# GpSimd instead of transfers for 80 low halves, one queue for the later transfers, and chunk ends taken bank by bank

## The chip, the cores and the metric

The kernel runs on one core of one Trainium2 chip. The metric is the device time of one execution in microseconds (us), median of three runs. The engines are TensorE (PE, with its weight loads as PEld), VectorE (DVE), ScalarE (ACT), GpSimd (POOL) and SyncE (SP). SP, ACT and POOL also issue the transfers (DMA), each in the order of its own queue.

## The reference, cut to what matters

One layer over 512 tokens of width 2048, in float32. `h = RMSNorm(x)` goes through one projection of width 13712 that feeds three branches and their gates. A is a sparse attention (an indexer picks 128 keys for each query, 8 heads), B a latent attention (8 heads, causal), C a cross-attention into 256 memory tokens (4 heads). Then:

```python
u = jnp.stack([o_a * silu(az), o_b * silu(bz), o_c * silu(cz)], axis=2)
y_br = jnp.einsum('bsnw,nwd->bsnd', u, w_branch[l])
g = jax.nn.sigmoid(gates.reshape(bsz, seq, N_BRANCH, d))
merged = jnp.einsum('bsnd,bsnd->bsd', g, y_br)
x = x + merged @ w_out[l]
```

## The kernel before, in words

**Halves.** Every large matmul is made from fp32r operands in two parts, a high half (the value rounded) and a low half (what the rounding left): high·high, high·low and low·high are summed, so each product is three matmuls. Activations are split once and kept; the weights are streamed in pieces of 128x1024 values (two rows of 128, 512 columns), called `wraw`, `sraw` or `so` when they land, and split into `whi` (an ACT copy) and `wlo` (source minus `whi`, on DVE). For the six silu-gate chunks of 512 columns (`w_in`, columns AZ, BZ, CZ; here "z chunks") and the first two of the three branch products, `wlo` is made otherwise (`halves_by_dma`): ACT writes minus `whi` into `wlo`, and a transfer on the POOL queue adds the same weights from DRAM to it (`accum_op`). There are 48 + 32 such pieces.

**The stream.** `stream` is the main line of matmuls. It walks jobs, one for each piece of weights: a plain chunk job is 2 rows x 4 banks x 3 = 24 matmuls of 512 columns, a Strassen job 12. Before a job's matmuls it prepares (`prep_upto`) up to three jobs ahead (`LOOK`), so `whi` and `wlo` have four buffers and `wraw` three, and issues on SP the load of the next piece whose buffer is let go. A plain chunk accumulates in the four banks of the ring `pg`; its last job ends them, `evac` empties each (ACT and DVE), and the next chunk opens the same four banks. Within a job the order is row, then bank.

**The order of the stages.** Memory keys and values, `iq0`, then the Strassen chunks of the projection and the merge gates (to about 878 us), `iq1`, the latent expansions `uq` and `ukv`, the z chunks, the branch products in the order C, B, A (`branch_chunk`, i = 0, 1, 2), and the output projection (`out_chunk`). Beside them run threads (`c_thread`, `c_part`, `b_thread`, `b_part`, `idx_thread`, `a_bias_thread`, `a_thread`, `u_thread`), Python generators that name what they wait for. All instructions are put in order at build time: `run` lets the stream emit a few matmuls and then lets each thread go on whose wait is over by the clock of `Plan`, a table of costs for each engine and queue. PE then executes that order strictly. A begins when B has ended (`a_bias_thread`, `a_prepare`: fourteen loads for positions, bias table, keys and values); the branch product i = 2 needs A's result through `u_thread` and `gate`.

**Queues.** Weight loads and the loads of `u_thread` are on SP. Spilled results (`to_dram`, `silu_to_dram`, `strassen_chunk`, `branch_chunk`) and the loads of the threads are on POOL; the stores of attention outputs (`sp_oA`, `sp_oB`, `sp_oC`) on ACT. The flag `gates` is set when `iq1` begins (`close_gates`).

Of the kernel before, what the change touches and what calls it, by code (L numbers as in the profile page):

```python
# [20 lines left out]
P = 128  # L21
# [35 lines left out]
class Engine:  # L57
# [6 lines left out]
    def __getattr__(self, name):  # L64
        f = getattr(self._eng, name)
        if name == "dma_start":
            q = "q_" + self._kind
            return lambda *a, **k: self._plan.call(f, q, name, a, k)
        if self._kind == "pool":
            return f  # L70
        return lambda *a, **k: self._plan.call(f, self._kind, name, a, k)


class Plan:
# [10 lines left out]
    def cost(self, kind, name, out, aps, accum):  # L85
# [153 lines left out]
class Kern:  # L239
# [34 lines left out]


# [49 lines left out]
    def stream(self):  # L325
# [29 lines left out]
        st = dict(nload=0, nprep=0, adds=[])  # L355
# [44 lines left out]
        def add_upto(n):  # L400
            while st["adds"] and st["adds"][0][0] <= n:
                st["adds"].pop(0)[1]()

        def halves(jb, src, w):
            h, l = new_pair()
            self.split(h[:, :, :w], l[:, :, :w], src)
            jb["hl"] = (h, l)

        def prep(jb):
            c, w = jb["c"], jb["cols"]  # L410
            if "kp" not in c or jb["ready"]:
                i, = jb["lids"]
                if c.get("dma"):
                    halves_by_dma(jb, raw[i])
                else:
                    halves(jb, raw[i][:, :, :w], w)
                done(i)
                return
            g, sh, p, kb = jb["g"], jb["sh"], jb["p"], jb["kb"]
            if p == "P1":  # L420
# [4 lines left out]
                halves(jb, g["11"], 512)  # L425
                tt(g["11"], g["12"], g["11"], op=OP.subtract)
            elif p == "P5":
                tt(sh["T2"][:, 2 * kb:2 * kb + 2], g["22"], g["11"], op=OP.subtract)
                halves(jb, g["11"], 512)
                done(g["ids"][0])  # L430
# [4 lines left out]
            elif p == "P7":  # L435
                halves(jb, g["12"], 512)
                done(g["ids"][1])
            elif p == "P2":
# [4 lines left out]
                halves(jb, g["21"], 512)  # L443
                done(g["ids"][0])
            elif p == "P4":
                halves(jb, sh["T2"][:, 2 * kb:2 * kb + 2], 512)
            else:
                halves(jb, g["22"], 512)
                done(g["ids"][1])
# [18 lines left out]
        for ji, jb in enumerate(jobs):  # L468
# [6 lines left out]
            add_upto(ji + self.LOOK - 1)  # L475
# [41 lines left out]
            for kk in range(2):  # L517
                k = jb["k"] + kk
                ah, al = c["act"](k)
                s, e = k == 0, k == c["nk"] - 1  # L520
                for b in range(c["nb"]):
                    p = c["ps"][b]
                    if c["mode"] == "tm":
                        n = c["cols"]
                        sl = slice(b * P, (b + 1) * P)
                        mm(p[:, :n], ah[:, sl], wh[:, kk, :n], start=s, stop=False)
                        mm(p[:, :n], ah[:, sl], wl[:, kk, :n], start=False, stop=False)
                        mm(p[:, :n], al[:, sl], wh[:, kk, :n], start=False, stop=e)
                    else:
                        m = min(P, c["cols"] - b * P)  # L530
                        sl = slice(b * P, b * P + m)
                        mm(p[:m], wh[:, kk, sl], ah, start=s, stop=False)
                        mm(p[:m], wh[:, kk, sl], al, start=False, stop=False)
                        mm(p[:m], wl[:, kk, sl], ah, start=False, stop=e)
                    if e:
                        c["evac"](b, p)
                    if kk == 1 and b == c["nb"] - 1:
                        jb.pop("hl")
                        if c.get("post") and e:
                            c["post"]()  # L540
                    yield
# [14 lines left out]
    def run(self, main, threads):  # L556
# [38 lines left out]
        for r in main:  # L595
# [5 lines left out]
            else:  # L601
                if self.later:
# [190 lines left out]
    def to_dram(self, key, nb, cols, scale=None, sums=()):  # L793
# [6 lines left out]
        def evac(b, p):  # L800
# [7 lines left out]
            else:  # L808
# [4 lines left out]
                nc.gpsimd.dma_start(dt[:, b - 1:b + 1], st[:, :, :cols])  # L813
# [13 lines left out]
    def silu_to_dram(self, key):  # L827
# [5 lines left out]
        def evac(b, p):  # L833
# [5 lines left out]
            if b % 2:  # L839
                nc.gpsimd.dma_start(dt[:, b - 1:b + 1], box["st"])  # L840
# [3 lines left out]
    def latent_thread(self):  # L844
# [3 lines left out]
        for i, (key, n, gain, (hi, lo)) in enumerate((("bcq", 512, self.g_bl, self.cqT),  # L848
# [3 lines left out]
            nc.gpsimd.dma_start(raw[:, :, :n], self.sp[key][:, :, :n])  # L852
# [16 lines left out]
    def kpe_thread(self):  # L869
# [5 lines left out]
        nc.gpsimd.dma_start(raw, self.sp["bckv"][:, :, 256:320])  # L875
# [34 lines left out]
    def c_thread(self):  # L910
        nc = self.nc
        yield "gates"
        with self.slots("cpool", side="right") as pool:
            def load(h):
# [5 lines left out]
                nc.gpsimd.dma_start(q, self.sp["cq%d" % c][:, :, sl])  # L920
                nc.gpsimd.dma_start(k, self.sp["ck%d" % c][:, :, sl])
                nc.gpsimd.dma_start(v, self.sp["cv%d" % c][:, :, sl])
# [48 lines left out]
    def c_part(self, t2):  # L971

        nc = self.nc
        for h in range(4):
# [44 lines left out]
            nc.scalar.dma_start(self.sp["oC%d" % c][:, 2 * j:2 * j + 2, t2 * 256:(t2 + 1) * 256], o)  # L1019
# [3 lines left out]
    def b_thread(self):  # L1023
# [4 lines left out]
        with self.slots("bpool") as pool:  # L1028
            self.flags.add("bpool")

            def load(h):
# [3 lines left out]
                nc.gpsimd.dma_start(q, self.sp["uq%d" % c][:, :, j * 192:(j + 1) * 192])  # L1035
                nc.gpsimd.dma_start(kv, self.sp["ukv%d" % c][:, :, j * 256:(j + 1) * 256])
# [64 lines left out]
    def b_part(self, tp):  # L1101

        nc = self.nc
        for h in range(8):
# [39 lines left out]
            nc.scalar.dma_start(self.sp["oB%d" % (h // 4)][:, h % 4, tp * 256:(tp + 1) * 256], o)  # L1144
# [3 lines left out]
    def idx_thread(self):  # L1148
# [6 lines left out]
        with self.slots("ipool") as pool:  # L1155
            ikw = pool.tile([P, NT, 80], F32, name="ikw")
            nc.gpsimd.dma_start(ikw, self.sp["bckv"][:, :, 320:400])
# [916 lines left out]
```

## Time and profile before

| | |
|---|---|
| median of 3 runs | 1891.43 us (1889.47 to 1894.97) |
| the profiled execution, its own time | 1891.4 us |
| its span, first to last instruction | 1889.6 us |
[...]
| PE busy, 9293 matmuls | 1850.9 us (98%) |
| DVE busy | 1323.3 us (70%) |
| ACT busy | 955.3 us (51%) |
| POOL busy | 278.4 us (15%) |
| share of the 16 DMA engines, queue of SP / POOL / ACT | 38.2% / 34.0% / 1.1% |

Busy PE is not PE at its peak, since matmuls overlap and their ends are modelled. "Idle" of a group of matmuls is the time in which PE did nothing just before them, and the releaser is the instruction that ended it. [...]

### The profile page before, as it was taken

How to read it: one execution, taken by the hardware profiler on the slowest of the kernel's cores; microseconds unless marked ns; L12 is line 12 of the kernel's file. 1: busy time of each engine (PE TensorE's matmuls, PEld its weight loads, DVE VectorE, ACT ScalarE, POOL GpSimd, SP SyncE). 2: the span in 40 equal slices, each digit the busy share in tenths (PEclk: the TensorE clock that was granted, in tenths of full speed). 3: DMA queues.
4: the chain of work that ended last, by engine and by line, in shares of the span. 5: the costliest groups of instructions: out<-in, count | busy, mean ns of one | idle time of the engine just before them, and what ended most of it. 6: DMA issues, size and time to landing. Idle time of an engine off the chain costs nothing.

```text
span 1889.6 us, 25158 instructions
## 1 busy us (share of the span) xinstructions
PE 1850.9 (98%) x9293; PEld 1539.8 (81%) x9293; DVE 1323.3 (70%) x2110; ACT 955.3 (51%) x1521; POOL 278.4 (15%) x344
## 2 busy tenths in 40 slices
PE   8999999999999999999999899999899999999999
PEld 6789888888888888888898788788678788887787
DVE  5478777778677777786654576886377786667655
ACT  6653554465444444443477576555444545334442
POOL 0100010100001100011113221212323232210000
PEclk9999999999999999999999999999999999999999
DMA  7854468867758697586468776879799999854784
GB/s 245 262 190 143 152 209 303 211 208 210 193 171 319 208 250 206 161 249 196 140 218 247 188 177 167 194 164 214 201 283 289 248 244 263 304 175 168 259 274 145
DMA packets 182380, 408.63 MB, mean 216 GB/s; under 512 B 15776, under 2 KB 28976, under 8 KB 180976
## 3 DMA queue, kind: packets, MB, share of 16 engines
q1 hardware_dynamic: 115152, 230.85, 38.2%
q0 software_dynamic: 58240, 169.87, 34.0%
q10 hardware_dynamic: 8864, 6.30, 1.1%
q8 instruction: 73, 1.20, 0.3%
q14 instruction: 51, 0.42, 0.1%
HBM read 348.47 MB, written 92.05 MB: 233 GB/s over the span
## 4 chain that ended last, share of the span: by engine, by line
PE 85%; DMA 5%; DVE 4%; ACT 4%; issue 2%; POOL 0%; ACTq 0%; DVEq 0%; POOLq 0%
PE pg L140 51%; PE pn L140 25%; PE pb L140 3%; PE pa L140 3%; DMA wraw<-w_mem_kv 2%; PE ra L140 2%; ACT whi L140 2%; DVE wlo L140 1%; PE rb L140 1%; ACT junk L140 1%; DMA stage<-sp_oB 1%; DMA b_q<-sp_uq 1%; DMA wlo<-w_in 1%; DVE stage L140 0%; ACT stage L140 0%
## 5 line engine op out<-in xcount | busy, mean ns | idle before, releaser
L140 ACT ACTIVATE whi<-wraw 128x1024 fp32r<-128x1024 f32 (+2 forms) x288 | 300.9, 1047 | 324.8 <-PE pg L140 155.1
L140 DVE TENSOR_TENSOR wlo<-wraw,whi 128x1024 fp32r<-128x1024 f32 (+2 forms) x208 | 250.2, 1205 | 150.9 <-ACT whi L140 149.6
L140 PE MATMUL pg<-whi,u 128*128 128x512 f32 x640 | 223.1, 403 | 3.9 <-DVE yg L140 1.9
L140 PE MATMUL pg<-hh,whi 128*128 128x512 f32 x512 | 210.1, 410 | 8.0 <-DVE stage L140 6.4
L140 PE MATMUL pg<-hh,wlo 128*128 128x512 f32 x512 | 202.2, 395 | 7.6 <-DMA wlo<-w_in 7.6
L140 PE MATMUL pg<-hl,whi 128*128 128x512 f32 x512 | 201.3, 393 | 0.0
L140 ACT ACTIVATE whi<-sraw 128x1024 fp32r<-128x1024 f32 x90 | 94.9, 1059 | 114.0 <-DVE sraw L140 54.6
L140 PE MATMUL pg<-whi,hS 128*128 128x512 f32 x448 | 147.0, 389 | 0.0
L140 DVE TENSOR_TENSOR wlo<-sraw,whi 128x1024 fp32r<-128x1024 f32 x90 | 109.9, 1224 | 50.5 <-ACT whi L140 49.8
L140 PEld LDWEIGHTS pg<-whi,u 128*128 128x128 f32 x640 | 121.0, 189 | 28.7 <-DVE yg L140 3.2
L140 PE MATMUL pn<-whi,hS 128*128 128x512 f32 x416 | 136.6, 389 | 0.0
L140 PE MATMUL pn<-whi,hl 128*128 128x512 f32 (+1 forms) x352 | 133.9, 380 | 0.0
L140 PE MATMUL pn<-wlo,hh 128*128 128x512 f32 (+1 forms) x352 | 133.9, 380 | 0.0
L140 PE MATMUL pn<-whi,hh 128*128 128x512 f32 (+1 forms) x352 | 133.9, 380 | 0.0
L140 PE MATMUL pg<-wlo,u 128*128 128x512 f32 x320 | 125.5, 392 | 0.0
L140 PEld LDWEIGHTS pg<-hh,wlo 128*128 128x128 f32 x512 | 97.0, 190 | 29.6 <-DMA wlo<-w_in 8.0
L140 PEld LDWEIGHTS pg<-hh,whi 128*128 128x128 f32 x512 | 97.5, 190 | 27.2 <-DVE stage L140 8.3
L140 DVE TENSOR_TENSOR wlo<-T,whi 128x1024 fp32r<-128x1024 f32 x72 | 88.0, 1222 | 40.4 <-ACT whi L140 40.1
L140 PE MATMUL pg<-wlo,hh 128*128 128x512 f32 x288 | 112.2, 389 | 0.0
L140 PE MATMUL pg<-whi,hl 128*128 128x512 f32 x288 | 112.1, 389 | 0.0
L140 PE MATMUL pg<-whi,hh 128*128 128x512 f32 x288 | 112.0, 389 | 0.0
L140 ACT ACTIVATE whi<-T 128x1024 fp32r<-128x1024 f32 x72 | 76.2, 1059 | 69.3 <-DVE T L140 25.2
(439 smaller groups left out, 4161.2 us busy)
## 6 DMA issues: line engine op xcount, KB each, us to landing
wraw<-w_in SPq DMA_DIRECT2D x154, 512.0 KB, 4.4
sraw<-w_in SPq DMA_DIRECT2D x90, 512.0 KB, 4.5
wT<-w_out POOLq DMA_DIRECT2D x24, 1024.0 KB, 19.9
wlo<-w_in POOLq DMA_DIRECT2D x48, 512.0 KB, 8.2
wraw<-w_branch SPq DMA_DIRECT2D x48, 512.0 KB, 5.9
wraw<-w_mem_kv SPq DMA_DIRECT2D x32, 512.0 KB, 5.5
wlo<-w_branch POOLq DMA_DIRECT2D x32, 512.0 KB, 9.1
yg<-sp_g POOLq DMA_DIRECT2D x24, 512.0 KB, 8.9
```

The source lines that it names most:

```text
L140: return f(*a, **k)
```

## The change

1. **GpSimd.** The transfers that add weights to `wlo` go, and so do ACT's copies of minus `whi`. In the z chunks and the branch products i = 0 and 1 GpSimd forms `wlo` with one `tensor_tensor` (source minus `whi`), emitted right behind `whi`, in POOL's queue. `Plan` counts such an operation as 100 + 2.1 ns for each column.
2. **Low halves apart.** Elsewhere DVE's `wlo` is no longer emitted right behind ACT's `whi` but held for one turn of the main line (Strassen and output chunks) or two (plain chunks), or until the next `whi` is emitted or the job is due. The piece's buffer counts as let go (`done`) from then on.
3. **Bank by bank.** In a chunk's first job and in its last the order is bank, then row: all six matmuls of a bank in sequence.
4. **SP.** From `gates` on, every transfer that was on POOL's or ACT's queue and isn't gone goes to SP's. Before `gates` they stay on POOL (the attention stores all come later).

```diff
-        if self._kind == "pool":
+        if self._kind == "pool" and name != "tensor_tensor":
...
+        if kind == "pool":
+            return 100 + 2.1 * n
...
+    def late_dma(self):
+        return (self.nc.sync if "gates" in self.flags else self.nc.gpsimd).dma_start
...
-        def halves_by_dma(jb, src):
-            h, l = new_pair()
-            nc.scalar.activation(h, src, AF.Copy)
-            nc.scalar.activation(l, h, AF.Copy, scale=-1.0)
-            jb["hl"] = (h, l)
-            (w,), row = jb["raws"][0]
-            st["adds"].append((st["nprep"], lambda: nc.gpsimd.dma_start(
-                l, w[row:row + 2 * P, :].rearrange("(k p) c -> p k c", p=P), accum_op=OP.add)))
...
+        def flush():
+            while st["lo"]:
+                st["lo"].pop(0)["f"]()
+
+        def tick():
+            for x in st["lo"]:
+                x["wait"] -= 1
+            if st["lo"] and st["lo"][0]["wait"] <= 0:
+                flush()
+        self.tick = tick
+
+        def halves(jb, src, w, ids=(), now=False):
+            h, l = new_pair()
+            h, l = h[:, :, :w], l[:, :, :w]
+            nc.scalar.activation(h, src, AF.Copy)
+            flush()
+            jb["hl"] = (h, l)
+            if jb["c"].get("pool"):
+                nc.gpsimd.tensor_tensor(l, src, h, op=OP.subtract)
+                done(*ids)
+                return
+
+            def low():
+                tt(l, src, h, op=OP.subtract)
+                done(*ids)
+            st["lo"].append(dict(f=low, wait=1 if "kp" in jb["c"] else 2, job=st["nprep"]))
+            if now:
+                flush()
...
-                halves(jb, g["11"], 512)
+                halves(jb, g["11"], 512, now=True)
                 tt(g["11"], g["12"], g["11"], op=OP.subtract)
...
+            if st["lo"] and st["lo"][0]["job"] <= ji:
+                flush()
...
-            for kk in range(2):
+            acts = [c["act"](jb["k"] + kk) for kk in range(2)]
+            order = [(kk, b) for kk in range(2) for b in range(c["nb"])]
+            if jb["first"] or jb["last"]:
+                order.sort(key=lambda x: x[1])
+            for kk, b in order:
...
             else:
+                self.tick()
                 if self.later:
...
-                nc.gpsimd.dma_start(dt[:, b - 1:b + 1], box["st"])
+                self.late_dma()(dt[:, b - 1:b + 1], box["st"])
...
-            nc.scalar.dma_start(self.sp["oA%d" % g][:, 2 * j:2 * j + 2, t * P:(t + 1) * P], o)
+            self.late_dma()(self.sp["oA%d" % g][:, 2 * j:2 * j + 2, t * P:(t + 1) * P], o)
...
-                self.chunks[-1]["dma"] = True
+                self.chunks[-1]["pool"] = True
...
-                self.chunks[-1]["dma"] = i < 2
+                self.chunks[-1]["pool"] = i < 2
```

## Rows read from the trace of the kernel before

**Rows 1.** Windows by stage: PE, PEld, DVE, ACT, POOL busy, PE clock, DMA, GB/s.

```profile
0.00:142.00 142.00, 133.35 (x607) 107.01 (x608) 85.39 (x139) 81.61 (x131) 14.39 (x26) 1.00 0.71 232
142.00:870.00 728.00, 727.50 (x3248) 607.87 (x3247) 560.29 (x516) 345.79 (x474) 56.94 (x73) 1.00 0.70 211
870.00:1005.00 135.00, 133.48 (x732) 118.06 (x731) 76.77 (x166) 81.55 (x210) 25.53 (x36) 1.00 0.62 201
1005.00:1345.00 340.00, 329.99 (x1708) 275.50 (x1708) 234.11 (x571) 211.93 (x376) 77.11 (x80) 0.99 0.79 191
1345.00:1387.00 42.00, 34.43 (x163) 27.94 (x163) 16.92 (x47) 15.58 (x18) 16.08 (x25) 0.92 0.87 237
1387.00:1633.00 246.00, 242.12 (x1723) 198.13 (x1722) 181.17 (x459) 117.59 (x191) 72.69 (x82) 0.99 0.94 265
...
1725.00:1890.00 165.00, 158.06 (x693) 129.16 (x691) 104.96 (x124) 66.27 (x73) 2.83 (x4) 0.99 0.62 205
```

**Rows 2.** Groups of PE instructions, by form: busy, mean ns; idle before, releasers.

```profile
L140 PE MATMUL pg<-whi,u 128*128 128x512 f32 x640 | 223.1, 403 | 3.9 <-DVE yg L140 1.9 <-DVE stage L140 1.9
L140 PE MATMUL pg<-hh,whi 128*128 128x512 f32 x512 | 210.1, 410 | 8.0 <-DVE stage L140 6.4 <-ACT stage L140 0.8 <-DVE u L140 0.8
L140 PE MATMUL pg<-hh,wlo 128*128 128x512 f32 x512 | 202.2, 395 | 7.6 <-DMA wlo<-w_in 7.6
```

**Rows 3.** Windows of 8 to 12 us around the longest stops, columns as in rows 1.

```profile
1074.00:1082.00 8.00, 5.14 (x20) 4.01 (x19) 6.53 (x11) 5.65 (x9) 3.14 (x5) 0.79 0.36 73
1153.00:1161.00 8.00, 5.96 (x22) 4.63 (x21) 5.10 (x8) 4.41 (x7) 4.44 (x5) 0.79 0.67 184
1362.00:1374.00 12.00, 5.72 (x18) 4.63 (x19) 8.86 (x35) 3.06 (x3) 3.59 (x6) 0.72 1.09 267
1389.00:1397.00 8.00, 6.11 (x35) 4.69 (x35) 6.87 (x12) 3.56 (x5) 3.09 (x4) 0.79 0.68 213
```

**Rows 4.** The chain that ended last, around 1074 us: start, length, what.

```profile
1071.22 1.06 ACT wlo L140
...
1077.41 0.69 DVE stage L140
...
1078.14 2.93 PE pg L140 x6
```

**Rows 5.** The same chain, a row of the Strassen chunks.

```profile
191.85 5.48 PE pg L140 x24
```

**Rows 6.** The same chain, around 1350 us.

```profile
1350.45 4.45 DMA pi<-positions
...
1358.29 9.95 DMA wlo<-w_in
```

**Rows 7.** Timeline of POOL from 1345 to 1370 us: start, busy, instruction.

```profile
1357.75 0.56 POOL L140 DMA_DIRECT2D akv<-sp_akv  x1
```

**Rows 8.** Timeline of ACT, same stretch; brackets hold idle before and releaser.

```profile
1365.71 1.06 ACT L140 ACTIVATE a_vh<-akv 128x1024 fp32r<-128x1024 f32 x1 [8.92 <-DVE pc L140]
```

**Rows 9.** Transfers by issue: KB each, median us from issue to landing.

```profile
wraw<-w_in SPq DMA_DIRECT2D x154, 512.0 KB, 4.4
...
akv<-sp_akv POOLq DMA_DIRECT2D x1, 1024.0 KB, 7.9
```

**Rows 10.** Timeline of all engines around 1630 us.

```profile
1629.10 1.23 DVE L140 TENSOR_TENSOR u<-stage,u 128x1024 fp32r<-128x1024 f32 x1 [1.13 <-ACT u L140]
...
1633.02 0.39 PE L140 MATMUL pn<-whi,u 128*128 128x512 f32 x1
```

**Rows 11.** Groups of ACT and DVE instructions: busy, mean ns; idle before, releasers.

```profile
L140 ACT ACTIVATE wlo<-whi 128x1024 fp32r<-128x1024 f32 x80 | 84.9, 1061 | 2.5
L140 DVE TENSOR_TENSOR wlo<-wraw,whi 128x1024 fp32r<-128x1024 f32 (+2 forms) x208 | 250.2, 1205 | 150.9 <-ACT whi L140 149.6
```

**Rows 12.** Groups of DVE instructions from 1380 to 1600 us, columns as in rows 11.

```profile
L140 DVE TENSOR_TENSOR a_st<-pq,pk 128x1024 bf16<-128x1024 f32 x40 | 48.6, 1217 | 0.0
```

**Rows 13.** Waits of SP's queue from 870 us on: total, times, longest.

```profile
SPq L140 <- ACT whi L140: 565.3, 80, 15.5
```

More of the change, by code (lines that the diff above doesn't have):

```diff
@@ L354, in stream @@
         raw = {}
-        st = dict(nload=0, nprep=0, adds=[])
+        st = dict(nload=0, nprep=0, lo=[])
         def load_some(most):
@@ L412, in prep @@
                 i, = jb["lids"]
[L413 to L417, printed above, removed]
+                halves(jb, raw[i][:, :, :w], w, [i])
                 return
@@ L428, in prep @@
                 tt(sh["T2"][:, 2 * kb:2 * kb + 2], g["22"], g["11"], op=OP.subtract)
-                halves(jb, g["11"], 512)
-                done(g["ids"][0])
+                halves(jb, g["11"], 512, g["ids"][:1])
             elif p == "P6":
@@ L435, in prep @@
             elif p == "P7":
-                halves(jb, g["12"], 512)
-                done(g["ids"][1])
+                halves(jb, g["12"], 512, g["ids"][1:2])
             elif p == "P2":
@@ L442, in prep @@
                 tt(t2, g["21"], t2, op=OP.subtract)
-                halves(jb, g["21"], 512)
-                done(g["ids"][0])
+                halves(jb, g["21"], 512, g["ids"][:1])
             elif p == "P4":
@@ L447, in prep @@
             else:
-                halves(jb, g["22"], 512)
-                done(g["ids"][1])
+                halves(jb, g["22"], 512, g["ids"][1:2])
         def prep_upto(n):
@@ L516, in stream @@
                 c["ps"] = [ring.bank([P, 512]) for _ in range(c["nb"])]
-            for kk in range(2):
+            acts = [c["act"](jb["k"] + kk) for kk in range(2)]
[3 more added lines that the diff above has]
+            for kk, b in order:
                 k = jb["k"] + kk
-                ah, al = c["act"](k)
+                ah, al = acts[kk]
                 s, e = k == 0, k == c["nk"] - 1
[L521 to L541, printed above, removed]
@@ new lines, in stream @@
+                p = c["ps"][b]
+                if c["mode"] == "tm":
+                    n = c["cols"]
+                    sl = slice(b * P, (b + 1) * P)
+                    mm(p[:, :n], ah[:, sl], wh[:, kk, :n], start=s, stop=False)
+                    mm(p[:, :n], ah[:, sl], wl[:, kk, :n], start=False, stop=False)
+                    mm(p[:, :n], al[:, sl], wh[:, kk, :n], start=False, stop=e)
+                else:
+                    m = min(P, c["cols"] - b * P)
+                    sl = slice(b * P, b * P + m)
+                    mm(p[:m], wh[:, kk, sl], ah, start=s, stop=False)
+                    mm(p[:m], wh[:, kk, sl], al, start=False, stop=False)
+                    mm(p[:m], wl[:, kk, sl], ah, start=False, stop=e)
@@ L543 @@
+                if e:
+                    c["evac"](b, p)
+                if (kk, b) == order[-1]:
+                    jb.pop("hl")
+                    if c.get("post") and e:
+                        c["post"]()
+                yield
     SLACK = (500.0, 300.0)
@@ L919, in load @@
                 v = pool.tile([P, 2, 256], F32, name="c_v", tag="c_v")
-                nc.gpsimd.dma_start(q, self.sp["cq%d" % c][:, :, sl])
-                nc.gpsimd.dma_start(k, self.sp["ck%d" % c][:, :, sl])
-                nc.gpsimd.dma_start(v, self.sp["cv%d" % c][:, :, sl])
+                self.late_dma()(q, self.sp["cq%d" % c][:, :, sl])
+                self.late_dma()(k, self.sp["ck%d" % c][:, :, sl])
+                self.late_dma()(v, self.sp["cv%d" % c][:, :, sl])
                 return q, k, v
@@ L1034, in load @@
                 kv = pool.tile([P, NT, 256], F32, name="b_kv", tag="b_kv")
-                nc.gpsimd.dma_start(q, self.sp["uq%d" % c][:, :, j * 192:(j + 1) * 192])
-                nc.gpsimd.dma_start(kv, self.sp["ukv%d" % c][:, :, j * 256:(j + 1) * 256])
+                self.late_dma()(q, self.sp["uq%d" % c][:, :, j * 192:(j + 1) * 192])
+                self.late_dma()(kv, self.sp["ukv%d" % c][:, :, j * 256:(j + 1) * 256])
                 return q, kv
@@ L1156, in idx_thread @@
             ikw = pool.tile([P, NT, 80], F32, name="ikw")
-            nc.gpsimd.dma_start(ikw, self.sp["bckv"][:, :, 320:400])
+            self.late_dma()(ikw, self.sp["bckv"][:, :, 320:400])
             def load(hp):
@@ L1161, in load @@
                 q = pool.tile([P, 512], F32, name="i_q", tag="i_q", bufs=2)
-                nc.gpsimd.dma_start(q, self.sp["iq%d" % c][:, j])
+                self.late_dma()(q, self.sp["iq%d" % c][:, j])
                 return q
@@ L1261, in a_prepare @@
         for s in range(4):
-            nc.gpsimd.dma_start(ki[s * 32:(s + 1) * 32], bass.AP(
+            self.late_dma()(ki[s * 32:(s + 1) * 32], bass.AP(
                 tensor=pos.tensor, offset=pos.offset + 32 * s, ap=[[0, 32], [P, NT], [1, 32]]))
-            nc.gpsimd.dma_start(rb[s * 32:(s + 1) * 32, 0], rel)
-            nc.gpsimd.dma_start(rb[s * 32 + 1:(s + 1) * 32, 1], rel[:31])
+            self.late_dma()(rb[s * 32:(s + 1) * 32, 0], rel)
+            self.late_dma()(rb[s * 32 + 1:(s + 1) * 32, 1], rel[:31])
         akv = pool.tile([P, NT, 512], F32, name="akv", tag="bm1", bufs=2)
-        nc.gpsimd.dma_start(akv, self.sp["akv"])
+        self.late_dma()(akv, self.sp["akv"])
         yield [pi, ki, rb, akv]
@@ L1358, in load @@
             q = til([P, 2, P], F32, "q", 2)
-            nc.gpsimd.dma_start(q, self.sp["aq%d" % g][:, t, j * 256:(j + 1) * 256])
+            self.late_dma()(q, self.sp["aq%d" % g][:, t, j * 256:(j + 1) * 256])
             return q
@@ L1725, in rest @@
                 if b % 2:
-                    nc.gpsimd.dma_start(self.sp["m%d" % i][:, b - 1:b + 1, cs], whole)
+                    self.late_dma()(self.sp["m%d" % i][:, b - 1:b + 1, cs], whole)
             self.defer(rest, b == 3, 1)
@@ L1801, in load @@
             box[i] = self.tp.tile([P, 2, 1024], F32, name="x_r", tag="m", bufs=2)
[L1802 removed]
+            self.late_dma()(box[i], x[:, 2 * i:2 * i + 2, cs])
         def put(i, j, t):
```

21 lines of the change are left out of this document (7 added, 14 removed).

## The prediction

> **What bounds the kernel now.** I read the windows by stage first. PE is the bound: from 142 to 870 us it is busy for 727.5 of 728 us [rows 1], so nothing that only relieves ACT, DVE or a queue can be worth anything there. What can be won lies behind 870 us. Subtracting PE's busy time from each window's length leaves 1.5 us idle up to 1005, 10.0 up to 1345, 7.6 up to 1387, 3.9 up to 1633 and 6.9 at the end [rows 1]. Idle at the very end is partly the last store.
>
> Next the groups of matmuls say who ended these stops. Two groups of plain chunk jobs waited 8.0 and 3.9 us for `stage`, `yg` and `u`: DVE or ACT emptying the four banks that the next chunk opens. One group waited 7.6 us, in one place, for the transfer that adds weights to `wlo` [rows 2].
>
> Then the clock. Four windows around the longest of these stops show 0.79, 0.79, 0.72 and 0.79 of full clock [rows 3]; time lost is length times the missing share: 8 x 0.21 = 1.7, 1.7, 12 x 0.28 = 3.4 and 1.7 us, together 8.5. [...]
>
> Last, the chain of work shows how each stop came about. At 1074 us an ACT `wlo` copy of 1.06 us stands in ACT's queue, several small splits of B follow, and DVE reaches the evacuation only at 1077.4 [rows 4]. At 1350 us POOL's queue reaches A's fourteen preparing loads at 1350.45 and is through with them, `akv` the last, at 1357.75 [rows 6, 7]; only then is the overdue addition to `wlo` issued, and takes 9.95 us [rows 6].
>
> **The change part by part.**
>
> *Bank by bank.* 24 matmuls take 5.48 us [rows 5], 0.228 each. In the old order bank 0 of a chunk's last job ends with matmul 15 and is opened again by matmul 25: nine matmuls, 2.05 us, for its evacuation, and the same for each bank. In the new order it ends with matmul 6 and is opened by 25: eighteen, 4.1 us. Every stop gets 2.05 us of room. The stop at 1074 is the longest: PE stood for 8.00 - 5.14 = 2.9 us [rows 3], so the evacuation came 2.05 + 2.9 = 5.0 us behind bank 0's last matmul. 0.9 us would stay, but the ACT copy of 1.06 that goes stood in that queue [rows 4]. So I take all 11.9 us (8.0 + 3.9) as gone. Bounds: nothing, if DVE's queue is late for other reasons, to 11.9. With them go the three 1.7 us of lower clock behind such stops.
>
> *Low halves on GpSimd.* This removes 80 ACT copies, 84.9 us [rows 11], off the path except in queues as above, and 80 transfers. With them goes the stop of 7.6 us and its 3.4 us of lower clock. Added are 80 subtractions of which the trace has no example. Below, DVE's 1.2 us for the same shape [rows 11]; above, the 9.95 us of the worst transfer replaced [rows 6]. `whi` is made up to three jobs, 16.4 us, ahead of its use, so even 9.95 us would be hidden once; but a job brings one such operation each 5.48 us, so beyond that POOL itself would set the pace. I take it to lie near DVE's value and cost nothing by itself, since POOL has nothing else to do by then. Its effect on DVE is a rival below.
>
> *SP.* POOL's and ACT's later transfers now stand in one queue with the weight loads. A weight load can be issued when the low half three jobs ahead is done, about 3 us into a job (1.06 for `whi`, 1.2 to 2.5 for `wlo`), takes 4.4 us to land [rows 9] and is wanted three jobs later: 16.4 - 7.9 = 8.5 us to spare. What blocks SP for less costs nothing; A's fourteen loads, 7.3 us on POOL [rows 6, 7], just fit. The other way round, a thread's transfer now stands behind a weight load that waits for its buffer: SP waited 565.3 us before 80 of them, 7.1 each [rows 13]. Threads mostly load one head ahead, so I count nothing, with 7 us a transfer as the upper bound; the point where it matters comes next.
>
> *Low halves apart.* DVE stood 149.6 us waiting for `whi` [rows 11], but mostly where PE was never short of work [rows 1]. Letting a buffer go one or two turns later (three matmuls each, 0.7 us) is covered by the 8.5 us. I count nothing; the 6.9 us of the last stage [rows 1] bound a gain, 1.4 us a job a loss where the cover is gone.
>
> *What is late next.* 11.9 + 7.6 + 8.5 = 28.0 us. But the third branch product needs A's end. Its first operand is ready at 1630.3 and PE starts on it at 1633.0 [rows 10]: 2.7 us to spare. The main line arrives there 28.0 us earlier. A starts earlier by what is saved ahead of 1345: 8.0 + 2 x 1.7 = 11.4. In its preparation ACT waited 8.9 us until `akv` let `a_vh` begin at 1365.7 [rows 8]; that transfer landed in 7.9 us, a half-size weight load on SP in 4.4 [rows 9], so 0 to 3.5 come back, and I take 2. Of the 3.9 + 1.7 us saved later, stops that hold A's matmuls too, I give A half, 2.8. A is then 16.2 us earlier, with its slack 18.9, and PE stands 28.0 - 18.9 = 9.1 us at the start of the third product. Bounds: 0 to 11.8 (A no faster than its start).
>
> Sum, on the profiled execution's own 1891.4 us, which is the median: 1891.4 - 28.0 + 9.1 = 1872.5.
>
> **The rivals.**
>
> *DVE is held up by GpSimd: slower.* While A runs, DVE is busy 181 of 246 us [rows 1], and A's comparisons, 40 of 1217 ns [rows 12], read two operands from SBUF as GpSimd's subtractions do. If DVE cannot run such an operation beside one of GpSimd's, each of the 32 there holds it by at least their own 1.2 us, 32 x 1.2 = 38 us on the thread that sets the third product's start: 1872.5 + 38 = 1911. It decides from 18.9 / 32 = 0.6 us of PE time for each. For it: the slack of 2.7 us; DVE is A's busiest engine. Against it: DVE is idle for 65 us in that stage, and operations that read PSUM, the evacuations among them, have one SBUF operand.
>
> [...]
>
> *A is not late: better.* In its stage ACT loses 32 copies, 34 of 117.6 busy us, and the DMA engines, 0.94 busy, lose 32 transfers [rows 1, 11]. If A gains 9.1 us by that, all 28.0 come: 1863.4, and 1857 with the output stage's stop.
>
> *Head of the line: about the same.* A's last store and the load of it behind a weight load each: 2 x 7.1 = 14.2 us more at the third product's start, 1886.7. For it: one queue for everything. Against it: the main line's order was made with that queue in `Plan`.
>
> *The evacuations stay late: the part does not do what it says.* DVE reaches them late because of what is queued ahead, not for want of banks. Then 11.9 + 5.1 stay, and 11.0 us saved at 1360 remain, less what A does not follow: 1880 to 1889.
>
> **How the numbers follow.** About 0.3%, 5.7 us, is what a measurement of this kernel can tell from no change. Forecast (1866 to 1880) 0.42; better (below 1866) 0.20; head of the line 0.12; late evacuations 0.10; slower 0.16. Of the head of the line and the late evacuations I give half to "faster" (below 1885.7) and half to "same": faster 0.42 + 0.20 + 0.11 = 0.73, same 0.11, slower 0.16. Predicted is the forecast, 1872.5. The range runs from 1857, the better case with all it can win, to 1894, beyond the two cases around no change, and leaves out about 0.05 below and 0.13 above.
>
> **What would show it.** Right: no PE wait on a `wlo` in the z chunks; the idle of the plain chunk groups, 8.0 and 3.9 before, near nothing; no lower clock from 1005 us to A's end; PE idle of some 9 us where the third product starts; the Strassen stage unchanged at 727.5 of 728. GpSimd's operations start to start can be no closer than a job, so their own length must be below 5.5 us. Wrong: DVE operations of the same form that got longer or began late beside GpSimd's; PE waiting for transfers of threads (`b_q`, `ikw`, `a_q`, `sp_oA`); weight loads landing late, seen as ACT waiting for `wraw`; new stops in the Strassen or memory stage, where I count nothing.

## The result and the profile after

The changed kernel takes 1908.6 us (1906.9 to 1910.3) against 1892.6 us for the kernel before beside it: a ratio of 1.0086, 95% interval 1.0067 to 1.0104. It is 0.9% slower; the forecast was 1872.5 us, and its range ended at 1894. The profiled execution took 1908.3 us, its span 1906.5, which is 16.9 longer than before.

The page of the kernel after, busy time of each engine:

```profile
PE 1852.2 (97%) x9293; PEld 1539.7 (81%) x9293; DVE 1392.9 (73%) x2110; ACT 873.9 (46%) x1441; POOL 274.8 (14%) x184
```

ACT lost its 80 copies (955.3 before, 873.9 now), as costed. DVE runs the same 2110 instructions, and they take 69.6 us more than the 1323.3 of before. That is the line to stop at: the change gives DVE no work.

Windows by stage after, columns as in [rows 1]:

```profile
142.00:870.00 728.00, 727.98 (x3251) 608.37 (x3251) 555.49 (x512) 348.94 (x475) 56.84 (x73) 1.00 0.67 211
870.00:1005.00 135.00, 130.40 (x705) 116.26 (x704) 74.11 (x160) 77.68 (x212) 9.36 (x6) 0.97 0.59 193
1005.00:1345.00 340.00, 318.60 (x1652) 262.30 (x1651) 274.96 (x573) 161.08 (x320) 93.90 (x39) 0.99 0.36 116
...
1408.00:1652.00 244.00, 236.95 (x1597) 194.41 (x1597) 186.79 (x408) 84.58 (x149) 76.49 (x29) 1.00 0.63 208
```

The Strassen stage is unchanged. From 870 to 1005 us PE is idle for 4.6 us (1.5 in [rows 1]), from 1005 to 1345 for 21.4 (10.0), in A's stage for 7.1 (3.9 in a window of similar length). The worst stage is that of B and the index heads, not A's; DVE is busy there for 275.0 us where it was 234.1, on hardly more instructions (573, 571 before).

The groups of PE instructions that answer to [rows 2]:

```profile
L142 PE MATMUL pg<-whi,u 128*128 128x512 f32 x640 | 219.7, 401 | 1.5 <-DVE yg L142 1.5
L142 PE MATMUL pg<-hh,whi 128*128 128x512 f32 x512 | 210.8, 412 | 2.9 <-DVE stage L142 2.9
L142 PE MATMUL pg<-hh,wlo 128*128 128x512 f32 x512 | 202.1, 395 | 0.0
```

So the three waits on which the forecast rested did go: 3.9 to 1.5, 8.0 to 2.9, 7.6 to 0. Others came. The waits of PE after, by what ended them (total, times, longest):

```profile
PE pb L142 <- DVE b_st L142: 5.3, 4, 1.9
PE pb L142 <- DVE b_pr L142: 5.1, 6, 2.1
PE pb L142 <- issue: 4.6, 1, 4.6
PE rb L142 <- issue: 3.9, 1, 3.9
...
PE rb L142 <- DVE bm L142: 3.2, 4, 1.6
PE pb L142 <- DVE b_pl L142: 3.1, 3, 1.5
```

These are products of the attention threads (`pb`, `rb` and the like are their banks in PSUM), waiting for DVE's softmax steps (`b_st`, `b_pr`, `bm`). No product waited for `u`, so A's end was not late. The groups of DVE instructions, busy and mean ns, say why:

```profile
L142 DVE TENSOR_TENSOR a_st<-pq,pk 128x1024 bf16<-128x1024 f32 x40 | 55.8, 1399 | 0.0
L142 DVE SCALAR_TENSOR_TENSOR sc<-i_r,iw,sc 128x256 f32<-128x256 f32 (+2 forms) x45 | 36.2, 817 | 4.8 <-ACT i_r L142 4.1
L142 DVE TENSOR_TENSOR b_pl<-pb,b_ph 128x128 fp32r<-128x128 f32 (+3 forms) x32 | 15.3, 485 | 14.7 <-ACT b_ph L142 14.6
L142 DVE TENSOR_TENSOR a_q<-a_q,a_rs 128x256 f32<-128x256 f32 x16 | 13.4, 842 | 0.6 <-DMA a_q<-sp_aq 0.6
L142 DVE TENSOR_TENSOR b_st<-b_st,b_rs 128x1 f32<-128x1 f32 x32 | 12.6, 395 | 1.1
```

Three of these groups before:

```profile
L140 DVE SCALAR_TENSOR_TENSOR sc<-i_r,iw,sc 128x256 f32<-128x256 f32 (+2 forms) x45 | 27.5, 615 | 23.2 <-ACT i_r L140 22.6
L140 DVE TENSOR_TENSOR b_pl<-pb,b_ph 128x128 fp32r<-128x128 f32 (+3 forms) x32 | 15.5, 488 | 19.8 <-ACT b_ph L140 19.7
L140 DVE TENSOR_TENSOR b_st<-b_st,b_rs 128x1 f32<-128x1 f32 x32 | 5.1, 160 | 1.1
```

`a_st` was 1217 ns [rows 12], `a_q` 418. `b_pl`, which reads one operand from PSUM, took 488 ns and takes 485. One tile at a time (duration min/median/max):

```profile
L142 POOL TENSOR_TENSOR wlo<-wraw,whi x80: 2361/2400/3493, 992.0 to 1627.7; 128x1024 fp32r<-128x1024 f32 x80
...
L142 DVE TENSOR_TENSOR b_st<-b_st,b_rs x32: 158/160/2308, 1034.5 to 1335.8; 128x1 f32<-128x1 f32 x32
...
L142 DVE TENSOR_TENSOR a_q<-a_q,a_rs x16: 404/413/2607, 1375.6 to 1584.8; 128x256 f32<-128x256 f32 x16
```

The medians are the old ones; the longest are about as long as one GpSimd subtraction. The timeline at 1041 us shows such a pair (a softmax step of C's thread, one column wide) and the product of B behind it:

```profile
1041.63 2.37 POOL L142 TENSOR_TENSOR wlo<-wraw,whi 128x1024 fp32r<-128x1024 f32 x1 [3.82 <-ACT whi L142]
...
1041.77 2.24 DVE L142 TENSOR_TENSOR c_st<-c_st,c_rs 128x1 f32<-128x1 f32 x1
...
1044.55 0.30 PE L142 MATMUL pb<-ident,b_pr 128*128 128x128 f32 x1 [1.88 <-DVE b_st L142]
```

GpSimd begins 0.14 us earlier; the DVE instruction is in execution until GpSimd's ends at 1044.00; then `b_st` and `b_pr` run, and PE, whose next instruction in its order this was, stood for 1.9 us. GpSimd can be the one that is held: at 1412 us `a_st` began first and took its usual time, and the subtraction beside it took 3.36 us:

```profile
1412.36 1.21 DVE L142 TENSOR_TENSOR a_st<-pq,pk 128x1024 bf16<-128x1024 f32 x1
1412.48 3.36 POOL L142 TENSOR_TENSOR wlo<-wraw,whi 128x1024 fp32r<-128x1024 f32 x1 [4.98 <-ACT whi L142]
```

The new stop of 4.6 us "by issue" is at 890 us, before any GpSimd subtraction:

```profile
885.50 0.34 SPq L142 DMA_DIRECT2D lraw<-sp_bcq  x1
...
890.30 0.39 PE L142 MATMUL pg<-hh,wlo 128*128 128x512 f32 x1
890.41 0.16 DVE L142 TENSOR_SCALAR l_v<-l_ss 128x4 f32<-128x4 f32 x1
...
892.79 2.29 DVE L142 TENSOR_TENSOR lraw<-lraw,l_rs 128x2048 f32<-128x2048 f32 x1
...
895.29 1.09 PE L142 MATMUL pb<-ident,lraw 128*128 128x128 f32 x4 [4.60 <-issue]
```

The transposes of `lraw` are in PE's order behind the product of 890.30, and DVE is only then at its thirteen steps ahead of them. From 893.1 us, inside that stop, to 900.0 the granted clock is 0.50; over the window of 890 to 898 us it is 0.70:

```profile
890.00:898.00 8.00, 3.40 (x14) 2.58 (x13) 7.45 (x22) 0.69 (x1) 0.00 (x0) 0.70 0.79 272
```

The clock is 0.79 in each of the 8 us windows from 1119, 1259 and 1365 us, around other stops: 0.50 for 3.4 us of each. The one at 1363.7 us is the other "by issue", 3.9 us: the transposes of `akv` stood behind DVE steps of A's preparation, of which `a_vv` took 2.38 us and `rs_t` 2.33, both beside GpSimd subtractions.

One wait came through the SP queue: the 1.5 us of `yg` in the groups above. SP could issue the load of `yg` only behind a weight load, and that one waited for a GpSimd subtraction that was itself held. From the chain that ended last:

```profile
1616.82 3.42 POOL wlo L142
...
1620.68 6.39 DMA yg<-sp_g
```

### The profile page after: what moved, and what is told of

Read it like the earlier page. It is cut to its first block, busy times and chain, and to the rows that moved or that the text cites. A ratio compares the mean times of both kernels' runs of the same rounds, so it can differ in the third digit from the quotient of the medians.

```text
span 1906.5 us, 25031 instructions
## 1 busy us (share of the span) xinstructions
PE 1852.2 (97%) x9293; PEld 1539.7 (81%) x9293; DVE 1392.9 (73%) x2110; ACT 873.9 (46%) x1441; POOL 274.8 (14%) x184
## 4 chain that ended last, share of the span: by engine, by line
PE 72%; DVE 12%; issue 7%; DMA 4%; ACT 2%; POOL 2%; SPq 0%; ACTq 0%; POOLq 0%; DVEq 0%
PE pg L142 41%; PE pn L142 25%; PE pb L142 2%; POOL wlo L142 2%; PE pa L142 2%; DMA wraw<-w_mem_kv 2%; DVE wlo L142 1%; DVE i_wk L142 1%; DVE b_st L142 1%; ACT whi L142 1%; DVE i_mx L142 1%; DVE a_st L142 1%; DVE stage L142 1%; DVE sc L142 1%; PE ra L142 1%
## 5 line engine op out<-in xcount | busy, mean ns | idle before, releaser
L142 POOL TENSOR_TENSOR wlo<-wraw,whi 128x1024 fp32r<-128x1024 f32 x80 | 201.2, 2516 | 544.0 <-ACT whi L142 538.0
L142 PEld LDWEIGHTS pg<-hl,whi 128*128 128x128 f32 x512 | 97.9, 191 | 16.0
```

The costliest lines, as they stand in the source:

```text
L142: return f(*a, **k)
```

## The experiments

The theory from the trace: **DVE is held up by GpSimd**. Against it stood: the order in which the threads are emitted, the one SP queue, the length of GpSimd's operation by itself. Kernels with "order kept" have the changed kernel's instructions on TensorE, VectorE and SP in the same order, since `Plan` was given the same cost. The other kernels have orders of their own, so that in a difference between one of them and the changed kernel the order plays a part too. The diffs are shortened: calls stand without the wrapper that gives `Plan` its cost.

| run | us | ratio to before, 95% |
|---|---|---|
| e1: low halves again by adding transfers | 1886.7 | 0.9963 to 0.9990 |
| e2: queues as before | 1919.6 | 1.0133 to 1.0163 |
| e3: GpSimd only writes zeros, order kept | 1866.2 | 0.9849 to 0.9882 |
| e4: subtraction in quarters, order kept | 1889.9 | 0.9978 to 1.0000 |
| e5: all low halves on DVE | 1902.5 | 1.0044 to 1.0076 |
| e6: GpSimd subtractions alone | 1922.8 | 1.0147 to 1.0175 |
| e7: bank order alone | 1887.5 | 0.9967 to 0.9986 |
| e8: e1, latents' loads on GpSimd's queue | 1887.8 | 0.9958 to 0.9986 |
| e9: adding transfers, order kept | 1900.5 | 1.0026 to 1.0056 |
| e10: gate paths on DVE, branches by adding | 1885.4 | 0.9951 to 0.9978 |
| e11: GpSimd copies, order kept | 1873.3 | 0.9889 to 0.9917 |
| e12: subtraction in eighths, order kept | 1891.4 | 0.9990 to 1.0008 |
| e13: zeros for 2.3 us, order kept | 1873.4 | 0.9878 to 0.9911 |
| e14: zeros for 3.8 us, order kept | 1882.2 | 0.9928 to 0.9958 |
| e15: e10, latents' loads on GpSimd's queue | 1899.4 | 1.0016 to 1.0045 |

**e1: without GpSimd's arithmetic.**

```diff
-                nc.gpsimd.tensor_tensor(l, src, h, op=OP.subtract)
+                nc.scalar.activation(l, h, AF.Copy, scale=-1.0)
+                st["adds"].append((st["nprep"], lambda: nc.gpsimd.dma_start(
+                    l, wd[row:row + 2 * P, :].rearrange("(k p) c -> p k c", p=P), accum_op=OP.add)))
```

> The changed kernel with its GpSimd subtractions taken back: ACT writes minus whi and a transfer on GpSimd's queue adds the weights, as before the change; bank by bank, the held low halves and the SP queue stay. If GpSimd's subtractions hold up DVE: the DVE forms that grew (b_st 128x1 from 160 to about 390 ns, a_q, sc) return to their lengths of before, and the time falls from 1908.6 to between 1870 and 1890. If threads' transfers stand too long in SP's queue: that queue is unchanged, so the time stays within 4 us of 1908.6.

1886.7 us, as expected; `b_st` 159 ns, `sc` 614, `a_q` 418. The other three parts of the change bring 4.5 us over before. Here A is late at the third product:

```profile
L142 PE MATMUL pn<-whi,u 128*128 128x512 f32 x128 | 43.2, 413 | 4.0 <-ACT u L142 2.1 <-DVE u L142 1.8
```

**e2: the queues back.**

```diff
-        return (self.nc.sync if "gates" in self.flags else self.nc.gpsimd).dma_start
+        return self.nc.gpsimd.dma_start
```

The stores of `oA`, `oB` and `oC` went back to ACT too.

> The changed kernel with its later transfers put back on GpSimd's and ACT's queues, GpSimd's subtractions kept. If GpSimd's subtractions hold up DVE: DVE's extra 70 us of busy time stay and the time stays between 1900 and 1915. If threads' transfers stand too long in SP's queue: PE's waits on the threads' matmuls go and the time falls to 1875 to 1890.

1919.6 us, above both expectations and 11 more than the changed kernel. DVE's extra busy time stayed (1408.1 us). So with the queues back, and the other order that comes with them, nothing is won: the one SP queue is not the fault. That transfers on GpSimd's queue stand behind subtractions of 2.4 us is the likely reason; no run took that by itself.

**e3: GpSimd writes and does not read.**

```diff
-                nc.gpsimd.tensor_tensor(l, src, h, op=OP.subtract)
+                nc.gpsimd.memset(l.bitcast(F32), 0.0)      # Plan told of the subtraction
```

> The changed kernel in its own order on every engine, with each of GpSimd's 80 subtractions replaced by writing zeros over the same 128x1024 tile; it leaves out the low halves of the weights in the gate chunks and in the first two branch products. If DVE operations with two SBUF operands are held by GpSimd instructions that read SBUF: DVE's lengths return to those of before (b_st 160 ns, sc 615 ns) and the time falls to 1865 to 1885. If any GpSimd instruction holds them: they stay long in proportion to the length of the writes. If the SP queue is the cause: the time stays within 4 us of 1908.6.

1866.2 us, 42.4 below the changed kernel in the same order. The tiles of GpSimd's work and of `b_st`:

```profile
L414 POOL MEMSET wlo<- x80: 948/954/1180, 986.8 to 1582.9; 128x1024 f32 x80
...
L142 DVE TENSOR_TENSOR b_st<-b_st,b_rs x32: 158/159/161, 1031.9 to 1306.0; 128x1 f32<-128x1 f32 x32
```

The lengths of DVE's operations with two operands are back (`sc` 613 ns, `a_q` 416), and in the window of B's stage PE is idle for 2.1 us where it was for 21.4:

```profile
1005.00:1345.00 340.00, 337.89 (x1806) 283.60 (x1805) 249.56 (x622) 169.90 (x326) 41.99 (x46) 1.00 0.42 129
```

The order is not at fault, nor are SP's queue and the bank order: all three are the same here. But this work is also shorter, and waits for neither `whi` nor `wraw`; e13 takes that up.

**e4 and e12: the same subtraction in pieces.**

```diff
-                nc.gpsimd.tensor_tensor(l, src, h, op=OP.subtract)
+                for at in quarters:                        # e12: eighths, 128 columns
+                    nc.gpsimd.tensor_tensor(l[at], src[at], h[at], op=OP.subtract)
```

> The changed kernel in its own order, each of GpSimd's subtractions cut into four of 128x256. If an operation of GpSimd holds DVE for its whole length: the longest hold falls from about 2.3 us to about 0.7, so a DVE operation of 160 ns is never seen above 1 us, and the time falls to 1880 to 1900. If DVE and GpSimd only share a rate: total time of both stays and so does the time, within 4 us of 1908.6. If the SP queue is the cause: the same, 1908.6.

> The changed kernel in its own order, with each GpSimd subtraction in eight of 128x128. The whole ones (2.40 us) held b_st, 160 ns long by itself, up to 2.31 us and gave 1908.6 us; quarters (0.74 us) held it up to 0.70 us and gave 1889.9. Theory "what counts is the length of one hold": a piece takes some 0.45 us, b_st is held up to about as long, VectorE's busy time falls below the 1364.5 us of the quarters, and the time below theirs: 1874 to 1886. Rival "what counts is the time that GpSimd reads SBUF in all": eighths make that longer (above 290 us), VectorE's busy time stays at or above that of the quarters, and the time is 1889 to 1900; a low half that comes too late through GpSimd's longer queue would show as stops of products for wlo.

Quarters, 1889.9 us; eighths, 1891.4. The tiles of e4:

```profile
L418 POOL TENSOR_TENSOR wlo<-wraw,whi x320: 712/740/1740, 991.1 to 1608.5; 128x256 fp32r<-128x256 f32 x160
...
L142 DVE TENSOR_TENSOR b_st<-b_st,b_rs x32: 158/159/700, 1033.5 to 1319.4; 128x1 f32<-128x1 f32 x32
```

And e12:

```profile
L418 POOL TENSOR_TENSOR wlo<-wraw,whi x640: 448/462/1540, 992.1 to 1613.4; 128x128 fp32r<-128x128 f32 x160
...
L142 DVE TENSOR_TENSOR b_st<-b_st,b_rs x32: 159/160/466, 1034.5 to 1315.1; 128x1 f32<-128x1 f32 x32
```

The longest `b_st` follows the length of one GpSimd instruction: 2308 ns at 2400, 700 at 740, 466 at 462. DVE's busy time follows too: 1392.9, 1364.5, 1349.3. The time does not fall with the eighths, whose 8 x 0.46 = 3.7 us are longer in all than 2.40; that expectation was missed, though its condition on DVE's busy time held.

**e13 and e14: as long as the subtraction, but writing.**

```diff
+                g.tensor_tensor(l[:, 0, :8], src[:, 0, :8], h[:, 0, :8], op=OP.subtract)
+                g.memset(l.bitcast(F32), 0.0)              # twice; e14: three and a half times
+                g.tensor_tensor(l[:, 1, 504:], src[:, 1, 504:], h[:, 1, 504:], op=OP.subtract)
```

> The changed kernel in its own order; each GpSimd subtraction becomes a subtraction of 8 columns, two writings of zeros over the tile, and a subtraction of 8 columns: about 2.4 us in all, waiting for whi at its start and holding wraw to its end as the subtraction did, but reading SBUF for a small part of it. The low halves of the weights are left out there but for 16 columns. Theory "the hold is all": VectorE's lengths stay near 160, 615 and 418 ns, and the time is that of the short writing-only work, 1866 to 1874. Rival "half of it is that low halves and buffers come later": 1882 to 1895, with lengths as before.

> The same with three and a half writings of zeros, about 3.8 us in all, as long as a subtraction in eighths. Theory "the hold is all": 1866 to 1876, so that the eighths' 1891.4 would be all hold. Rival "length counts": above the run of 2.4 us by 5 us or more, 1880 to 1895, near the eighths.

Their length is 2 x 0.95 + 2 x 0.20 = 2.3 us and 3 x 0.95 + 0.53 + 0.40 = 3.8 us. e13 gave 1873.4 us, in the range of "the hold is all"; e14 1882.2, in that of "length counts". The tile of `b_pr` on DVE, one source in SBUF, no longer than 0.64 us before, and of `b_st`, in e13:

```profile
L142 DVE TENSOR_SCALAR b_pr<-b_pr,b_st x32: 285/420/1244, 1038.4 to 1310.3; 128x128 f32<-128x128 f32 x8, 128x384 f32<-128x384 f32 x8, 128x256 f32<-128x256 f32 x8, 128x512 f32<-128x512 f32 x8
...
L142 DVE TENSOR_TENSOR b_st<-b_st,b_rs x32: 159/159/161, 1033.0 to 1308.9; 128x1 f32<-128x1 f32 x32
```

GpSimd was busy for 105.2 of the 340 us from 1005 to 1345, where these 32 `b_st` are, and none of them took over 161 ns. So at nearly equal length the reading costs 1908.6 - 1873.4 = 35.2 us, and the eighths' 1891.4 - 1882.2 = 9.2. The other 7.2 us (e3 to e13) and 8.8 (e13 to e14) come with GpSimd's length: low halves and `wraw`'s buffers come later, and beside GpSimd's writing some of DVE's one-source SBUF operations are still held (`b_pr` to 1244 ns, `c_pr` to 1187; 637 and 526 before). Which of the two weighs more was not told apart.

**e11: one source.**

```diff
-                nc.gpsimd.tensor_tensor(l, src, h, op=OP.subtract)
+                nc.gpsimd.tensor_copy(l, src)              # Plan told of the subtraction
```

> The changed kernel in its own order, with GpSimd copying wraw into wlo (one source in SBUF) where it subtracted: the weights' low halves are left out of the products there. Theory "any reading by GpSimd holds VectorE's operations with two SBUF sources and its fast copies": b_st, sc and a_q grow again (b_st above 250 ns, a_q above 550), and the time lies between that with writing-only work and the changed kernel by the length of the copy: 1878 to 1905. Rival "only GpSimd's two-source operations hold": lengths of before (160, 615, 418 ns) and 1863 to 1870.

1873.3 us, between the two expectations. Here `wlo` holds a copy of the weights, where e3 and e13 write zeros; so it is not the zeros that make those two fast. `b_st` is held again, by less than the copy's 1.05 us, and too seldom for the expected means (`b_st` 196 ns, `a_q` 507):

```profile
L414 POOL CAST wlo<-wraw x80: 1032/1046/2084, 987.8 to 1591.4; 128x1024 fp32r<-128x1024 f32 x80
...
L142 DVE TENSOR_TENSOR b_st<-b_st,b_rs x32: 158/159/811, 1033.7 to 1313.4; 128x1 f32<-128x1 f32 x32
```

**e5, e9, e10: other places for the low halves.** e5 sets `pool` to false everywhere, e10 for the gate paths, with e1's adding transfers for the branches; e9 is e1's pair of operations at the place of the subtraction, `Plan` being given the cost of the subtraction.

> The changed kernel with the 80 subtractions on VectorE instead of GpSimd: same emission apart from the high halves, same SP queue, same bank order. Theory "VectorE held up by GpSimd": lengths of VectorE's short operations return to those of before (b_st 160 ns, sc 615 ns, a_q 418 ns), VectorE's busy time is 1323 + 80 x 1.2 = about 1419 us, more than the 1393 of the changed kernel; the time is nevertheless below the changed kernel's 1908.6, since a subtraction of 1.2 us sits in the queue where 2.4 us of GpSimd's held a chain: 1885 to 1903, with 1895 as the value. Rival "VectorE is full": what counts is its busy time, so the time is that of the changed kernel or above it: 1909 to 1925.

> The changed kernel with its instruction order on TensorE, VectorE and SP kept, and each of the 80 GpSimd subtractions replaced by ScalarE's negative copy and an adding transfer on GpSimd's queue, issued at once. Theory "VectorE held up by GpSimd": no operation of VectorE is longer than before (b_st 160 ns, sc 615 ns, a_q 418 ns), and the time falls from 1908.6 towards that with writing-only GpSimd work (1866.2); late adding transfers (7.6 us before) and ScalarE's 80 added copies give some of it back: 1866 to 1880, value 1872. Rival "the adding transfers cost as much as the hold": 1886 to 1900, with stops of products for wlo.

> The changed order with the low halves of the gate paths on VectorE and those of the two branch products by adding transfers. The run with all low halves on VectorE had few stops between 1000 and 1340 us and one of 24 us in all around the start of the third product, where A was late; the runs with adding transfers had A late by 0 to 4 us. Theory "A is late when VectorE carries more in its stage": the stop at the third product is under 5 us, the stage of B as in the run on VectorE: 1874 to 1884, value 1879. Rival "A is late from what was put off in B's stage": the stop at the third product is over 10 us, 1890 to 1900.

e5 gave 1902.5 us, as expected: DVE does the same work in 1.2 us each and is busy for 1408.2 us, `b_st`, `sc` and `a_q` have their lengths of before, and the kernel is 6 us below the changed one (the intervals just overlap). B's stage has no more stops than in e3, in e5's window of it:

```profile
1005.00:1345.00 340.00, 338.71 (x1775) 284.27 (x1774) 282.23 (x621) 166.46 (x322) 0.21 (x2) 1.00 0.41 126
```

A pays, being late at the third product; the longest waits of PE in e5:

```profile
PE pn L142 <- ACT u L142: 7.7, 1, 7.7
PE pg L142 <- ACT u L142: 5.5, 1, 5.5
```

e9 gave 1900.5 us, 20 above its upper expectation and at the rival's upper end, though `b_st` took 160 ns. The rival's sign is missing too: no product waited for an adding transfer. Other transfers came late: PE's longest wait is 5.2 us for `yg`, and `a_q` landed in 7.4 us (3.6 in the changed kernel). The DMA engines were busy for 0.79 of the time from 1005 to 1345 us and 0.97 from 1408 to 1652 (0.36 and 0.63 in the changed kernel); that the other transfers came late because of the adding ones is likely, not shown. e1, with the same work issued at other moments and in its own order, took 13.8 us less. e10 gave 1885.4 us, 1.4 above its expectation, 0.35% below before and the lowest of those with the whole computation, if not clearly below e1; its products of `u` waited 5.9 us in all, so A still set part of the time.

**e6 and e7: one part alone on the kernel before.** e6 replaces the ACT copy and the adding transfer by the GpSimd subtraction; e7 is the bank order (`order.sort` for the first and last jobs of four-bank groups).

> The kernel before with one part of the change alone: the 80 low halves by a GpSimd subtraction right behind the high half, transfers and bank order as before. Theory "VectorE held up by GpSimd": the hold (42 us between the changed kernel and the one with writing-only GpSimd work) comes, less the 7.6 us of the waits for adding transfers that go, and the waits of products for VectorE's evacuations (8.7 us before) grow: 1915 to 1932, with 1922 as the value; b_st above 300 ns, a_q above 600 ns. Rival "it takes the new order with it": the hold matters only together with the later low halves and the one queue, and alone the subtractions give 1882 to 1895.

> The kernel before with the bank order alone (the one two-bank group at the start left as it was). Theory (the prediction's term for late evacuations): the wait of products for whi after VectorE's evacuation, 8.0 us before, falls to about 3, and half-clock stretches behind those stops become fewer: 1878 to 1887, value 1883. Rival "evacuations stay late": the stop moves to another wait of the same products, 1889 to 1894.

e6: 1922.8 us, as expected. e7: 1887.5, above its upper value by 0.5. Its groups of PE:

```profile
L140 PE MATMUL pg<-whi,u 128*128 128x512 f32 x640 | 219.8, 401 | 0.0
L140 PE MATMUL pg<-hh,whi 128*128 128x512 f32 x512 | 208.7, 408 | 0.0
L140 PE MATMUL pg<-hh,wlo 128*128 128x512 f32 x512 | 201.6, 394 | 8.2 <-DMA wlo<-w_in 8.2
...
L140 PE MATMUL pn<-whi,u 128*128 128x512 f32 x128 | 42.4, 406 | 11.0 <-ACT u L140 11.0
```

Both waits for evacuations are gone, 11.9 us to 0, and 11.0 us come back in one stop at the third product, for `u`, which A's end lets begin.

**e8 and e15: the stop at 890.** In e1 and e10 the three loads of the latents are issued on GpSimd's queue again, which `Plan` counts as later.

> The kernel of adding transfers on the changed order (1886.7), with the three loads of the latents (both lraw, kpe_raw) issued on GpSimd's queue as before. Theory "SP brings the stop at 890": the stop of 5 us ahead of the transposes of lraw goes, with the stretch at the lower clock behind it (3.4 us lost): 1876 to 1881, value 1878. Rival "the stop comes from the order of the emission, not from the queue": the stop stays, 1885 to 1889.

> Low halves of the gate paths on VectorE, those of the two branch products by adding transfers (1885.4), and the three loads of the latents on GpSimd's queue again. Theory "the stop at 890 is a cost of its own": it goes, with the lower clock behind it, and nothing else comes: 1875 to 1880. Rival "A gives it back at the third product": 1882 to 1887, with A's stops longer by as much.

The stop went in both, and no time with it: 1887.8, in the rival's range without the rival's condition, and 1899.4, outside both. The threads behind it were emitted elsewhere, and new stops came: in e8 6.1 us for `akv` and 5.7 for `u`, in e15 7.9 us for `u` at the third product and 6.0 for an evacuation. That a stop ahead of 1005 us is worth only what A's end lets through would fit both; no run shows it by itself.

## Why the prediction was wrong, step by step

- **The step that failed** is "Low halves on GpSimd": "I take it to lie near DVE's value and cost nothing by itself". Two things were wrong in it. Its length is 2.40 us, not near 1.2; the change's own line in `Plan`, 100 + 2.1 x 1024 = 2250 ns, would have said so. And its effect on DVE, left to a rival with 0.16, is the largest term of all: of the 42.4 us between e3 and the changed kernel 35.2 come with the reading (e13), the rest with the length.
- **The rival was right in mechanism, not in place, and its 1911 came near by luck.** It priced 32 of A's comparisons at 1.2 us, on the thread that sets the third product's start. Those grew by 40 x 0.18 = 7.3 us in all, and they ran earlier than before, so A set nothing there. Before, after and in e3:

```profile
L140 DVE TENSOR_TENSOR a_st<-pq,pk x40: 1210/1217/1221, 1381.5 to 1566.1; 128x1024 bf16<-128x1024 f32 x40
L142 DVE TENSOR_TENSOR a_st<-pq,pk x40: 1205/1213/3424, 1374.4 to 1553.8; 128x1024 bf16<-128x1024 f32 x40
L142 DVE TENSOR_TENSOR a_st<-pq,pk x40: 1207/1215/1221, 1338.9 to 1509.2; 128x1024 bf16<-128x1024 f32 x40
```

The hold was spread over DVE's operations with their operands in SBUF, one column wide or a thousand, and cost most in B's stage (PE idle 21.4 us for 10.0), where A's slack does not come in: B's products stand in PE's own order, so a late softmax step stops PE on the spot.

- **Which operations are held was a guess.** The rival took two operands in SBUF as the condition, and the rows of before have no GpSimd arithmetic to show it. In the changed kernel operations with one source in SBUF are held too (`b_pr` to 2374 ns, 637 before), and in e13, where GpSimd writes but for 16 columns, `b_pr` to 1244. In the two pairs above, at 1041 and 1412 us, it is the operation that began second that grew: `c_st`, 160 ns by its median, to 2.24 us, and the subtraction, 2.40 by its median, to 3.36. The 2.5 us that "SP" has as the upper value for `wlo` was an estimate that no row of before shows; measured are 1.2 on DVE and 2.40 on GpSimd.
- **"Bank by bank" was right.** 11.9 us to 0 in e7. In the changed kernel 4.4 stay: 1.5 for `yg`, whose load was late, and 2.9 for `stage`. Ahead of the longest of these, 1.5 us at 1290 us, DVE had a held step (`ro_x`, 1.60 us); the others' cause was not followed.
- **The 7.6 us for the adding transfer went**, as costed. The 8.5 us of the lower clock did not: the old windows went, others came behind the new stops, and the mean granted clock is 0.995 before and after. In e3, which has fewer stops, it is 0.998.
- **"What is late next", 9.1 us at the third product, was right as a mechanism and wrong in size.** e7 has 11.0 us, e1 4.0, e3 none. In e3 the third product starts at 1604.6 us, 28.4 ahead of the 1633.0 of before; the sum had 28.0. But A's first comparison is 42.6 us ahead, where the sum gave A 16.2 in all. So there all of the gain came: 1866.2, near the 1863.4 of "A is not late". How much of A's gain is the SP queue, how much the 32 copies and 32 transfers that went, no run told apart.
- **"SP" at nothing** was half right. It brought the stop of 4.6 us at 890, which is gone where the latents' loads are back on GpSimd's queue (e2, e8, e15), but e8 and e15 show that removing it pays nothing. The head of the line shows little in PE's waits: 1.0 us for a transfer behind 870 us (`ikw`), and the 1.5 us through `yg`.
- **"Low halves apart" at nothing**: no run told it apart.

Without the hold the forecast's range would have held: 1866.2 (e3) and 1873.4 (e13) lie in it. That e13 comes within 1 us of 1872.5 is luck: the 9.1 us at the third product are not there, and the stop at 890 and the length of GpSimd's work, which are, were not in the sum. The range failed because the rival was given one chance in six, on the argument that DVE is idle for a quarter of A's stage and that evacuations read PSUM. DVE's idle time does not help a chain in which PE waits for the very step that is held.

## What to carry to other kernels

Before moving elementwise work to GpSimd, list the DVE operations that will run beside it and have their operands in SBUF: here `b_st`, 160 ns by itself, was held up to 2308 beside subtractions of 2400, and a hold in a chain that feeds TensorE became a stop (1.9 us of PE at 1044 us). If it must be, make the pieces short (quarters won back 19 of the 42 us here) and keep them out of stages with short dependent DVE chains; writing-only work of nearly the same length cost 35 us less here. And a saving on the main line is worth only what the side thread behind it lets through: look for the next point where the two meet, and test the part alone.

## What the runs showed of the hardware

- A DVE instruction of one column (`b_st`, 160 ns) lasted up to 2308 ns with GpSimd subtractions of 2400 (median), 700 and 466 with pieces of 740 and 462, 811 with GpSimd copies of 1046, and 161 with GpSimd writing zeros (e3, e13). With the zeros of e13 a DVE operation with one source in SBUF, `b_pr`, still took up to 1244 ns: 637 before, and 487 in e15, where GpSimd does no arithmetic.
- The hold goes the other way too: a GpSimd subtraction (median 2400 ns) took 3360 where it began behind an `a_st` of 1210 on DVE.
- `b_pl`, a DVE operation with one operand in PSUM, was not held: 488 ns before, 485 after, the longest 692 in both.
- GpSimd's subtraction took 2400 ns for 1024 columns, 740 for 256, 462 for 128 and 202 for 8, so by an estimate from these medians about 2.2 ns a column and 0.2 us for each instruction. Zeros took 954 ns for 1024 columns.
